# Float32r transposes of copied queries and keys, and probabilities transposed one step later

## The chip, the cores and the metric

The kernel runs on one core of one Trainium2 chip. The metric is the device time of one execution in microseconds; the program before takes 460.76 us (median of 3 runs, 460.70 to 461.07). TensorE, VectorE, ScalarE, GpSimd and SyncE are called PE, DVE, ACT, POOL and SP below, as in the profile.

## What is computed

One layer of a hybrid decoder: 512 tokens of width 1024, float32. A normalised input goes through one wide projection, whose columns feed a block-sparse attention branch (8 heads of 64) and a gated linear recurrence (4 heads of 128); both are up-projected, gated, merged, projected again, and a gated embedding is added.

```python
xn = rmsnorm(h, norm_gain[i])
proj = xn @ w_in[i]
aq, ak, av, ag, bq, bf, bi, bg, gate_a, gate_b = jnp.split(proj, split_pts, axis=-1)
qa = rmsnorm(heads(aq), q_norm_gain[i])
ka = rmsnorm(heads(ak), k_norm_gain[i])
ya = moba_attention(qa, ka, heads(av), rel_bias)      # softmax(q k^T * scale + bias) v, causal
ya = (ya * silu(ag)) @ w_up_a[i]
yb = hgrn2_chunkwise(silu(bq), kb, bi, log_f)
yb = (rmsnorm(yb, hgrn_out_gain[i]) * silu(bg)) @ w_up_b[i]
h = h + (sigmoid(gate_a) * ya + sigmoid(gate_b) * yb) @ w_out[i]
h = h + (p[i] @ w_ple[i]) * sigmoid(h @ w_ple_gate[i])
```

## The kernel before

Each large product is made of float32r matmuls on operands that are split in a high and a low part (hi·hi, hi·lo, lo·hi), 128x128 weights against 512 columns. `proj_tr` and `mm3` (L256) make one 128-row block of the projection from 24 such matmuls; `proj_tok` (L396) makes the value, query and key projections with tokens on partitions, in four PSUM banks of 128 tokens each: `bi`, `av`, `aq`, `ak`. Weights come by SP's transfers, ACT writes their high part (`wh`, L239) and DVE the low part (`wl`, L240), three buffers each.

The main stream on PE is a list of such blocks (`ORDER`): after `aq` and `ak` come `bg0`, `ag0`, `bf1`, `bq1`, `bg1` and so on, then `ub`, `ua`, `h` and the last gate. Into this stream side generators put their own work: the recurrence (score matmuls `lpb` and `lpa`, transposes `hktp`, state products `hds`, outputs `hop`), the normalisation of queries and keys (`qk_norm`), and attention. The stream counts estimated microseconds (`tick`, `cost`), and a generator that yields a number gets its turn when the count has passed it. PE's order is therefore the order in which the code is written out (`manual_schedule` for PE). ACT, DVE and POOL get their order from a scheduler that simulates the program at build time.

PSUM has four banks for the main stream (tag `mm`), two for the recurrence (`g`) and two for attention (`a`). The four `mm` banks go round: `ak0` to `ak3` hold the key projection, and `bg0`, `ag0`, `bf1`, `bq1` are written into those same banks, each after its `ak` has been copied out.

`qk_norm`, for queries and then for keys: ACT copies each bank to a tile (`qr` or `kr`, L636), squares it (`qq`, `kq`, L638), DVE sums the squares (L639), ACT and DVE make the inverse root (L267 to L272), DVE multiplies the tiles in place (L645). The raw query tiles stand in the buffers `P` and `PC` that attention uses later, the raw key tiles in `R`, which has four buffers of its own. PE transposes them as float32: four 128x128 transposes for each pair of heads, `qtp` (L658) four times in a row of turns, `ktp` (L674) once for each pair of heads as attention gets to it. Column 0 of the bias tiles of the first two heads is first written from the last key tile (L764), so that their load comes no sooner.

Attention has 24 steps (8 heads, query blocks (0, 1), (2), (3)). A step's scores (`s`, L700) go to one `a` bank; DVE adds the bias and takes the row maximum (L707), ACT exponentiates (L709). In the next step `divide` scales the probabilities (ACT, L722), and a transfer on ACT's queue copies them to a float32r tile (`pc`, L726). `LAG` steps after its scores, at 0.4 of the step, PE transposes `pc` (`pt`, L734), ACT copies the result (`ptS`, L738), and each pair of heads ends with the products with the values (`o`, L749).

The recurrence's end for head 0 matters below: PE makes `hop0` (L595, L597), ACT squares it (`ht0`, L603), and `column_norms` makes the norm: a transpose and a reduction on DVE (L332, L333), four small DVE operations (L334 to L337), the logarithm and exponential on ACT (`n16t` L267, `n16y` L268), more on DVE, and the output `ho0` (L605), which stands in a ring of eight buffers, `YB`.

Of the kernel before, what the change touches and what calls it, by code (L numbers as in the profile page):

```python
# [11 lines left out]
F32 = mybir.dt.float32  # L12
R = mybir.dt.float32r
# [8 lines left out]
NT = S // 128  # L22
# [8 lines left out]
STEPS = ((0, 1), (2,), (3,))  # L31

HP = 3.1
AP = 6.1
LAG = 2
H0 = 8.0
XN = 3.0

# [22 lines left out]
def hybrid_layer_kernel(  # L61
    ctx: ExitStack,
    tc: tile.TileContext,
    xT: bass.AP,
    pT: bass.AP,
    smalls: bass.AP,
    brow: bass.AP,
    masks: bass.AP,
    w_tok: bass.AP,
    w_tr: bass.AP,  # L70
# [6 lines left out]
    nc = tc.nc  # L77
    V, A, G, PE = nc.vector, nc.scalar, nc.gpsimd, nc.tensor
# [11 lines left out]
    def unit(tag, name, dt=F32, shape=(128, 512)):  # L90
        return sb.tile(list(shape), dt, tag=tag, bufs=BUFS[tag], name=name)

    def bank(tag, name):
        return psum.tile([128, 512], F32, tag=tag, bufs={"mm": 4, "g": 2, "a": 2}[tag], name=name)
# [34 lines left out]
    def cost(us):  # L129
        now[0] += us  # L130
# [26 lines left out]
    identr = cst.tile([128, 128], R, name="identr")  # L157
    G.tensor_copy(identr, identf[:, 0:128])
    ident = identr.bitcast(F32)
# [27 lines left out]
    def pin(op, engine="V"):  # L187

        if engine in pinned:
            tc.add_manual_dep(op.ins, pinned[engine].name,  # L190
                              mybir.DependencyInfo(mybir.DependencyClass.NoSync, mybir.DependencyReason.DATA))
        pinned[engine] = op.ins
# [5 lines left out]
    def scale_split(hi, lo, src, g):  # L198
        A.activation(hi, src, AF.Copy, scale=g)
        V.scalar_tensor_tensor(lo, src, g, hi.bitcast(F32), op0=OP.mult, op1=OP.subtract)  # L200
# [64 lines left out]
    def rsqrt(y, t, ms):  # L265

        A.activation(t, ms, AF.Ln, bias=epsc[0:t.shape[0], 0:1])  # L267
        A.activation(y, t, AF.Exp, scale=-0.5)  # L268
        V.scalar_tensor_tensor(t, ms, EPS, y, op0=OP.add, op1=OP.mult)
        V.tensor_tensor(t, t, y, op=OP.mult)  # L270
        V.tensor_scalar(t, t, -0.5, 1.5, op0=OP.mult, op1=OP.add)
        V.tensor_tensor(y, y, t, op=OP.mult)  # L272
# [356 lines left out]
    def qk_norm(name, banks, g, res):  # L629
        raws = []  # L630
        ss = cst.tile([128, NT, HEADS], F32, name=name + "ss")
        y = cst.tile([128, NT, HEADS], F32, name=name + "y")
        t_ = cst.tile([128, NT, HEADS], F32, name=name + "t")
        for t in range(NT):
            raw = unit(("P", "PC")[t % 2] if name == "q" else "R", f"{name}r{t}")
            A.activation(raw, banks[t], AF.Copy)  # L636
            sq = unit("PT", f"{name}q{t}")
            A.activation(sq, raw, AF.Square)  # L638
            V.tensor_reduce(ss[:, t], sq.rearrange("p (h d) -> p h d", h=HEADS), axis=AX.X, op=OP.add)  # L639
            raws.append(raw)  # L640
        V.tensor_scalar(ss, ss, 1.0 / 64, None, op0=OP.mult)
        rsqrt(y, t_, ss)
        for t in range(NT):
            r3 = raws[t].rearrange("p (h d) -> p h d", h=HEADS)
            V.tensor_tensor(r3, r3, y[:, t, :, None].to_broadcast([128, HEADS, 64]), op=OP.mult)  # L645
        yield 14.0
        if name == "q":
            yield from stacked_queries(raws, g, res)
        else:
            res.extend(raws)  # L650
        done.add(name)

    def stacked_queries(raws, g, res):

        for i in range(HPAIRS):
            tp = bank("a", f"qtp{i}")
            for t in range(NT):
                PE.transpose(tp[:, t * 128:t * 128 + 128], raws[t][:, i * 128:i * 128 + 128], ident)  # L658
            cost(0.44)
            with tc.high_priority(offset=AHEAD):  # L660
                for j in range(2):
                    qs = unit("A", f"qs{2 * i + j}", R)
                    own, other = slice(64 * j, 64 * j + 64), slice(64 - 64 * j, 128 - 64 * j)
                    A.activation(qs[own], tp[own], AF.Copy, scale=g[own])
                    V.scalar_tensor_tensor(qs[other], tp[own], g[own], qs[own].bitcast(F32),
                                           op0=OP.mult, op1=OP.subtract)
                    res.append(qs)
            yield 1.5

    def doubled_keys(raws, i):  # L670

        tp = bank("a", f"ktp{i}")
        for t in range(NT):
            PE.transpose(tp[:, t * 128:t * 128 + 128], raws[t][:, i * 128:i * 128 + 128], ident)  # L674
        cost(0.44)
        res = []
        for j in range(2):
            kh = unit("A", f"kh{2 * i + j}", R)
            kl = unit("A", f"kl{2 * i + j}", R)
            own, other = slice(64 * j, 64 * j + 64), slice(64 - 64 * j, 128 - 64 * j)  # L680
            with tc.high_priority(offset=AHEAD):
                scale_split(kh[own], kl[own], tp[own], kgain[own])
            for k_ in (kh, kl):
                nc.sync.dma_start(k_[other].bitcast(F32), k_[own].bitcast(F32))
            res.append((kh, kl))
        return res

    def attention(qn, kraw, va, sags, res):
# [24 lines left out]
        def divide(n):  # L713


            if n not in prs:
                return
            with tc.high_priority(offset=AHEAD):
                for _, st in scaled:
                    pin(V.reciprocal(st[:, 2:3], st[:, 1:2]))  # L720
                for p_, st in scaled:
                    A.activation(p_, p_, AF.Copy, scale=st[:, 2:3])  # L722
                h, i = steps[n]
                w = 128 * sum(qb + 1 for qb in STEPS[i])
                c = unit("PC", f"pc{h}{i}", R)
                nc.scalar.dma_start(c[:, 0:w].bitcast(F32), prs[n][:, 0:w])  # L726
                prs[n] = c
            scaled.clear()

        def transposed(h, qbs, pr):  # L730
            n = sum(qb + 1 for qb in qbs)
            tp = bank("a", f"pt{h}{qbs[0]}")
            for kb in range(n):
                PE.transpose(tp[:, kb * 128:kb * 128 + 128].bitcast(R), pr[:, kb * 128:kb * 128 + 128], identr)  # L734
            cost(0.06 * n)
            pt = unit("PT" if n == NT else f"PT{qbs[0]}", f"ptS{h}{qbs[0]}", shape=(128, n * 128))
            with tc.high_priority(offset=AHEAD):
                A.activation(pt, tp[:, :n * 128], AF.Copy)  # L738
            return pt
# [21 lines left out]
        def bias(h):  # L761
            t = unit("T", f"bias{h}")
            if h < 2:
                V.tensor_copy(t[:, 0:1], kraw[NT - 1][:, 0:1])  # L764
            row = brow[h:h + 1, :]
            nc.sync.dma_start(t, bass.AP(tensor=row.tensor, offset=row.offset, ap=[[1, 128], [1, 512]]))
            return t

        while not {"q", "k"} <= done:
            yield lambda: {"q", "k"} <= done  # L770
        T = {0: bias(0), 1: bias(1)}
        kn += doubled_keys(kraw, 0)
        yield 7.0
        NS = len(STEPS)
        steps = [(h, i) for h in range(HEADS) for i in range(NS)]
        prs, pts = {}, {}
        pending = None
        for n in range(len(steps) + LAG + 1):
            divide(n - 1)
            if pending is not None:  # L780
                while f"ag{pending}" not in done:
                    yield lambda: f"ag{pending}" in done
                out_values(pending, pts)
                pending = None
            if n < len(steps):
                h, i = steps[n]
                prs[n] = scores(h, STEPS[i], T[h])
                if i == 1 and h + 2 < HEADS:
                    T[h + 2] = bias(h + 2)
                if i == 1 and h % 2 and h + 1 < HEADS:  # L790
                    yield 1.0
                    kn += doubled_keys(kraw, h // 2 + 1)
                yield AP * (0.4 if n >= LAG else 0.8)
            if LAG <= n < len(steps) + LAG:
                h, i = steps[n - LAG]
                pts[h, i] = transposed(h, STEPS[i], prs.pop(n - LAG))
                if i == NS - 1 and h % 2:
                    pending = h // 2
                yield AP * 0.6

    def drain(name):

# [245 lines left out]
    for at, n in enumerate(PAIRS):  # L1048
# [24 lines left out]
        if at in (2, 3):  # L1073
            t = unit("A", f"pf{at}")
# [12 lines left out]
    for p in range(4):  # L1087
        pes = [bank("ag"[p % 2], f"pe{p}{i}") for i in range(2)]
        a, b, c, d = (bank("mm", f"g{i}{p}") for i in "abcd")
# [186 lines left out]
```

## Time and profile before

| | |
|---|---|
| runs | 460.70, 460.76, 461.07 us |
| profiled execution | 461.04 us, of which the span from the first to the last instruction is 459.0 us |
| mean granted TensorE clock | 0.999 |
| PE busy | 99% of the span |
| DVE busy | 74% |
| ACT busy | 64% |
| DMA | 55.69 MB, mean 121 GB/s |

The profile was taken from one execution. Busy time counts from an instruction's start to its end; matmuls overlap, so the pace of PE is read from the starts: the 512-column matmuls of the main stream start 0.23 us apart. In the timelines a row has the start, the duration, the engine, the line and operation, output<-inputs, shapes, a count, and in brackets the engine's idle time before it and what ended that.

### The profile page before, as it was taken

The numbers are of one execution on the slowest core, as the hardware profiler recorded it, in microseconds if no ns is written. First come the engines' busy times: TensorE is split into PE (matmuls) and PEld (weight loads), VectorE is DVE, ScalarE is ACT, GpSimd is POOL, SyncE is SP. The second block draws the span as 40 slices with busy tenths as digits, with TensorE's granted clock in tenths as the row PEclk, the third lists the DMA queues.
The fourth block names the chain that finished last, engine by engine and source line by source line (L and its number), as shares of the span: only waits on it lengthen the run. The fifth ranks groups of instructions, "written<-read, shape, count | busy, mean of one in ns | idle before, by whom it ended". The sixth has DMA issues, their size and how long they took to land.

```text
span 459.0 us, 7767 instructions
## 1 busy us (share of the span) xinstructions
PE 453.2 (99%) x2903; PEld 383.1 (83%) x2903; DVE 341.4 (74%) x715; ACT 294.3 (64%) x538; POOL 14.3 (3%) x35
## 2 busy tenths in 40 slices
PE   8999999999999999999999999999999999999996
PEld 6888888888888888888878888888888888899996
DVE  4889567869979877978897556233548968899885
ACT  5856665658688987979696866766434435557331
POOL 1005000000000000001000000000000000000000
PEclk9999999999999999999999999999999999999999
DMA  7642322321443533442523344213423534463112
GB/s 253 213 142 78 107 91 95 99 84 57 158 131 112 158 106 133 131 134 88 160 89 124 119 125 162 63 64 109 133 92 111 175 129 161 160 202 120 47 47 93
DMA packets 23061, 55.69 MB, mean 121 GB/s; under 512 B 2800, under 2 KB 5744, under 8 KB 23024
## 3 DMA queue, kind: packets, MB, share of 16 engines
q1 hardware_dynamic: 19424, 49.95, 33.8%
q10 hardware_dynamic: 3600, 5.25, 3.1%
q8 instruction: 23, 0.38, 0.3%
q14 instruction: 14, 0.11, 0.1%
HBM read 45.75 MB, written 2.10 MB: 104 GB/s over the span
## 4 chain that ended last, share of the span: by engine, by line
PE 96%; DMA 2%; ACT 1%; issue 0%; DVE 0%; SPq 0%; DVEq 0%
PE ga L256 10%; PE gb L256 10%; PE h L256 10%; PE ub L256 5%; PE ak L396 5%; PE bq L256 5%; PE ua L256 5%; PE ag L256 5%; PE bf L256 5%; PE aq L396 5%; PE av L396 5%; PE bi L396 4%; PE bg L256 4%; PE pe L1103 2%; PE ga L1112 2%; PE gc L1112 2%
## 5 line engine op out<-in xcount | busy, mean ns | idle before, releaser
L240 DVE TENSOR_TENSOR wl<-wf,wh 128x1024 fp32r<-128x1024 f32 (+1 forms) x70 | 77.6, 1110 | 39.4 <-ACT wh L239 38.3
L239 ACT ACTIVATE wh<-wf 128x1024 fp32r<-128x1024 f32 (+1 forms) x70 | 67.1, 959 | 58.8 <-PE h L256 9.8
L256 PE MATMUL gb<-xh,wh 128*128 128x512 f32 x64 | 25.8, 403 | 0.0
L256 PE MATMUL ga<-xh,wh 128*128 128x512 f32 x64 | 25.6, 400 | 0.0
L256 PE MATMUL gb<-xh,wl 128*128 128x512 f32 x64 | 25.1, 392 | 0.0
L256 PE MATMUL ga<-xh,wl 128*128 128x512 f32 x64 | 25.0, 391 | 0.0
L256 PE MATMUL gb<-xl,wh 128*128 128x512 f32 x64 | 25.0, 391 | 0.0
L256 PE MATMUL ga<-xl,wh 128*128 128x512 f32 x64 | 25.0, 390 | 0.0
L256 PE MATMUL h<-ml,wh 128*128 128x512 f32 x64 | 25.0, 390 | 0.0
L256 PE MATMUL h<-mh,wl 128*128 128x512 f32 x64 | 24.9, 389 | 0.0
L256 PE MATMUL h<-mh,wh 128*128 128x512 f32 x64 | 24.9, 389 | 0.0
L707 DVE CUSTOM_DVE_ANT_0 p<-s,bias 128x128 f32<-128x128 f32 (+3 forms) x32 | 15.0, 486 | 11.5 <-PE s L700 10.9
L709 ACT ACTIVATE p<-p,ps 128x128 f32<-128x128 f32 (+3 forms) x32 | 17.7, 555 | 7.4 <-DVE ps L707 7.2
L722 ACT ACTIVATE p<-p,ps 128x128 f32<-128x128 f32 (+3 forms) x32 | 17.0, 553 | 6.4 <-DVE ps L720 6.3
L738 ACT ACTIVATE ptS<-pt 128x384 f32<-128x384 f32 (+1 forms) x24 | 12.5, 520 | 6.6 <-PE pt L734 6.4
L256 PEld LDWEIGHTS h<-ml,wh 128*128 128x128 f32 x64 | 12.0, 188 | 2.7 <-DVE ml L196 0.2
L256 PEld LDWEIGHTS gb<-xh,wl 128*128 128x128 f32 x64 | 12.0, 188 | 2.7
L256 PEld LDWEIGHTS ga<-xh,wl 128*128 128x128 f32 x64 | 12.0, 188 | 2.7
L256 PEld LDWEIGHTS h<-mh,wh 128*128 128x128 f32 x64 | 12.0, 188 | 2.5
L256 PEld LDWEIGHTS h<-mh,wl 128*128 128x128 f32 x64 | 12.0, 188 | 2.4
L256 PEld LDWEIGHTS ga<-xh,wh 128*128 128x128 f32 x64 | 12.0, 187 | 2.3
L256 PEld LDWEIGHTS ga<-xl,wh 128*128 128x128 f32 x64 | 12.0, 188 | 2.2
(412 smaller groups left out, 1406.7 us busy)
## 6 DMA issues: line engine op xcount, KB each, us to landing
wf<-in_w_tr_dram SPq DMA_DIRECT2D x32, 512.0 KB, 3.3
wf<-in_w_tok_dram SPq DMA_DIRECT2D x15, 512.0 KB, 3.3
wf<-in_w_up_dram SPq DMA_DIRECT2D x16, 256.0 KB, 2.6
wf<-in_w_o_dram SPq DMA_DIRECT2D x8, 512.0 KB, 3.3
pc<-p ACTq DMA_DIRECT2D x16, 192.0 KB, 2.8
bias<-in_brow_dram SPq DMA_DIRECT2D x8, 256.0 KB, 3.8
pc<-p ACTq DMA_DIRECT2D x8, 256.0 KB, 2.7
xres<-in_xT_dram SPq DMA_DIRECT2D x8, 256.0 KB, 3.1
```

The costliest lines, as they stand in the source:

```text
L239: A.activation(hi, wraw[i], AF.Copy)
L240: pin(V.tensor_tensor(lo, wraw[i], hi.bitcast(F32), op=OP.subtract))
L256: PE.matmul(ps, a[:, k, :], b[k], start=(n == 0), stop=(n == tot - 1))
L396: PE.matmul(banks[t], a[:, s_], b[:, kk, :], start=(k == 0 and i == 0), stop=(k == KD - 1 and i == 2))
L707: V.tensor_tensor_reduce(p_, sp[:, o:o + nk], T[:, nk - 1::-1], -1.0, 3e38, OP.add, OP.min, st[:, 0:1])
L709: A.activation(p_, p_, AF.Exp, bias=st[:, 0:1], scale=-1.0, accum_out=st[:, 1:2])
L722: A.activation(p_, p_, AF.Copy, scale=st[:, 2:3])
L738: A.activation(pt, tp[:, :n * 128], AF.Copy)
L1103: PE.matmul(pes[i][:, cols], wt[:, i, k, :], t[k][:, cols], start=k == n == 0, stop=k == 1 and n == 2 and (bool(parts) or cols == right))
L1112: PE.matmul(dst[:, left], wt[:, k, :], bt, start=begin and n == 0, stop=n == 11, skip_group_check=not begin)
```

## The change

There are two parts.

1. **Queries and keys.** The raw tiles `qr` and `kr` move to the ring `YB` (eight buffers, four for each of the two). After the multiplication by the inverse root, a transfer on ACT's queue copies each tile to a float32r tile: `qc` in `P` and `PC`, `kc` in `R`, where the raw tiles were. The transposes read these copies, with the float32r identity, and write a float32r view of the bank. The tile that gates the first two bias loads is now `kc3`.
2. **Attention's order.** `LAG` goes from 2 to 3, and the transposes of probabilities stand at the head of a step, ahead of the division and the scores, with no turn of the main stream between them and the scores. `AP`, the counted length of a step, goes from 6.1 to 6.4.

```diff
-AP = 6.1
-LAG = 2
+AP = 6.4
+LAG = 3
...
         for t in range(NT):
-            raw = unit(("P", "PC")[t % 2] if name == "q" else "R", f"{name}r{t}")
+            raw = unit("YB", f"{name}r{t}")
...
             V.tensor_tensor(r3, r3, y[:, t, :, None].to_broadcast([128, HEADS, 64]), op=OP.mult)
+            c = unit(("P", "PC")[t % 2] if name == "q" else "R", f"{name}c{t}", R)
+            nc.scalar.dma_start(c.bitcast(F32), raws[t])
+            raws[t] = c
...
-                PE.transpose(tp[:, t * 128:t * 128 + 128], raws[t][:, i * 128:i * 128 + 128], ident)
-            cost(0.44)
+                PE.transpose(tp[:, t * 128:t * 128 + 128].bitcast(R), raws[t][:, i * 128:i * 128 + 128], identr)
+            cost(0.24)
...
-                V.tensor_copy(t[:, 0:1], kraw[NT - 1][:, 0:1])
+                V.tensor_copy(t[:, 0:1], kraw[NT - 1][:, 0:1].bitcast(F32))
...
         for n in range(len(steps) + LAG + 1):
-            divide(n - 1)
             if pending is not None:
...
+            if LAG <= n < len(steps) + LAG:
+                h, i = steps[n - LAG]
+                pts[h, i] = transposed(h, STEPS[i], prs.pop(n - LAG))
+                if i == NS - 1 and h % 2:
+                    pending = h // 2
+            divide(n - 1)
             if n < len(steps):
...
-                yield AP * (0.4 if n >= LAG else 0.8)
-            if LAG <= n < len(steps) + LAG:
-                h, i = steps[n - LAG]
-                pts[h, i] = transposed(h, STEPS[i], prs.pop(n - LAG))
-                if i == NS - 1 and h % 2:
-                    pending = h // 2
-                yield AP * 0.6
+                yield AP * (1.0 if n >= LAG else 0.8)
+            else:
+                yield AP * 0.5
```

The same edit of the transposes stands in `stacked_queries` (queries) and `doubled_keys` (keys). What the order of the engines makes of this is shown at three places. The line numbers of the changed kernel are 3 to 4 higher than those of before from L645 on.

On ACT, before, at the end of the key projection: the copies of the key banks `ak0` to `ak2` (`kr0` to `kr2`) stand between the query tiles `qs`, ahead of `ht0`.

```order
L636 ACTIVATE kr0_1139<-ak0_786 128x512
L664 ACTIVATE qs4_1052<-qtp2_1047,qgain_92 64x512
L638 ACTIVATE kq0_1141<-kr0_1139 128x512
L636 ACTIVATE kr1_1144<-ak1_787 128x512
L664 ACTIVATE qs5_1055<-qtp2_1047,qgain_92 64x512
L664 ACTIVATE qs6_1077<-qtp3_1072,qgain_92 64x512
L638 ACTIVATE kq1_1146<-kr1_1144 128x512
L636 ACTIVATE kr2_1149<-ak2_788 128x512
L664 ACTIVATE qs7_1080<-qtp3_1072,qgain_92 64x512
L638 ACTIVATE kq2_1151<-kr2_1149 128x512
L603 ACTIVATE ht0_1098<-hop0_1089 128x512
L239 ACTIVATE wh20_1128<-wf20_1126 128x1024
```

The same place on ACT now:

```order
L667 ACTIVATE qs7_1088<-qtp3_1080,qgain_92 64x512
L603 ACTIVATE ht0_1109<-hop0_1100 128x512
L239 ACTIVATE wh20_1136<-wf20_1134 128x1024
L267 ACTIVATE n16t_109<-n16s_107,epsc_79 32x16
L268 ACTIVATE n16y_108<-n16t_109 32x16
L636 ACTIVATE kr0_1147<-ak0_786 128x512
L636 ACTIVATE kr1_1152<-ak1_787 128x512
L636 ACTIVATE kr2_1157<-ak2_788 128x512
L636 ACTIVATE kr3_1162<-ak3_789 128x512
L638 ACTIVATE kq0_1149<-kr0_1147 128x512
```

All four copies of key banks now stand behind `n16t` and `n16y` of the recurrence's norm. In the program `kr0` itself waits for nothing; the first matmul into `bg0` waits for ACT's count up to and with `kr0`, whose bank it takes.

On DVE now, the operations that make the input of `n16t`, from the transpose of `ht0` on, with the low part of weight block 20 among them:

```order
L332 STREAM_TRANSPOSE h0nu_1111<-ht0_1109 128x512
L333 TENSOR_REDUCE n16s_107<-h0nu_1111 128x16
L240 TENSOR_TENSOR wl20_1137<-wf20_1134,wh20_1136 128x1024
L334 TENSOR_TENSOR n16s_107<-n16s_107 32x16
L335 TENSOR_TENSOR n16s_107<-n16s_107 32x16
L336 TENSOR_TENSOR n16s_107<-n16s_107 32x16
L337 TENSOR_SCALAR n16s_107<-n16s_107 32x16
L269 SCALAR_TENSOR_TENSOR n16t_109<-n16s_107,n16y_108 32x16
```

Before, two operations on the squares of keys (`kss`) stood between these; they now come behind `ho0`.

On PE, around the transposes of the probabilities of head 3, query block 2 (`pt32`), before: they stand 12 main-stream matmuls behind the scores of their second next step, and alone.

```order
L256 MATMUL bg3_2537<-xl7_412,wh36_2390 128x512
L256 MATMUL bg3_2537<-xh7_411,wl36_2391 128x512
L734 MATMUL pt32_2591<-identr_88,pc31_2488 128x128 x3
L256 MATMUL ag3_2608<-xh0_380,wh37_2468 128x512
L256 MATMUL ag3_2608<-xl0_381,wh37_2468 128x512
```

The same place now:

```order
L256 MATMUL bg3_2569<-xl4_399,wh36_2406 128x512
L256 MATMUL bg3_2569<-xh4_398,wl36_2407 128x512
L737 MATMUL pt32_2598<-identr_88,pc31_2429 128x128 x3
L703 MATMUL s42_2610<-kh4_2341,qs4_1060 128x384
L703 MATMUL s42_2610<-kl4_2342,qs4_1060 128x384
L256 MATMUL bg3_2569<-xh5_402,wh36_2406 128x512
```

They now stand directly ahead of the scores of the third next step. From the scores at whose step the division was made (`s33`) to `pt32` there were 42 main-stream matmuls, one score group and one group of transposes; now there are 54, with a score group, a group of transposes and the `hop` products.

More of the change, by code (lines that the diff above doesn't have):

```diff
@@ L673, in doubled_keys @@
         for t in range(NT):
-            PE.transpose(tp[:, t * 128:t * 128 + 128], raws[t][:, i * 128:i * 128 + 128], ident)
-        cost(0.44)
+            PE.transpose(tp[:, t * 128:t * 128 + 128].bitcast(R), raws[t][:, i * 128:i * 128 + 128], identr)
+        cost(0.24)
         res = []
```

## The prediction

> **What bounds the kernel now.** I read the busy times and the chain of the page first, then the waits of PE.
>
> ```profile
> PE 453.2 (99%) x2903; PEld 383.1 (83%) x2903; DVE 341.4 (74%) x715; ACT 294.3 (64%) x538; POOL 14.3 (3%) x35
> ...
> PE 96%; DMA 2%; ACT 1%; issue 0%; DVE 0%; SPq 0%; DVEq 0%
> ```
>
> ```profile
> PE pt L734 <- DMA pc<-p: 0.8, 1, 0.8
> ```
>
> PE works all the time: 96% of the chain is PE, and behind the first microseconds its waits hold one idle stretch, before transposes of probabilities. So an edit counts by what it does to PE's sequence of starts: a shorter instruction is a gain, and a wait of PE is a loss in full, because no idle time comes later that could take it up.
>
> **The change part by part.**
>
> *Type of the transposes.* 32 transposes go from float32 to float32r, in eight groups of four. Neither kind is new to the trace. A group of keys (`ktp`) as it is, and a group of four probabilities (`pt`), each between 512-column matmuls:
>
> ```profile
> 125.21 0.40 PE L256 MATMUL bf<-xh,wl 128*128 128x512 f32 x1
> 125.44 0.60 PE L674 MATMUL ktp<-identr,kr 128*128 128x128 f32 x4
> 125.80 0.48 PE L256 MATMUL bf<-xh,wh 128*128 128x512 f32 x1
> 126.11 0.40 PE L256 MATMUL bf<-xl,wh 128*128 128x512 f32 x1
> ```
>
> ```profile
> 189.33 0.40 PE L256 MATMUL ag<-xh,wl 128*128 128x512 f32 x1
> 189.56 0.46 PE L734 MATMUL pt<-identr,pc 128*128 128x128 f32 x4
> 189.86 0.46 PE L256 MATMUL ag<-xh,wh 128*128 128x512 f32 x1
> 190.16 0.40 PE L256 MATMUL ag<-xl,wh 128*128 128x512 f32 x1
> ```
>
> From the matmul ahead of the group to the second one behind it: 126.11 - 125.21 = 0.90 us in float32, 190.16 - 189.33 = 0.83 us in float32r. The difference, 0.075 us before rounding of the starts, times eight is **-0.60 us**, about 0.30 of it in the four query groups, which all stand ahead of `bg0`. (The program's own estimates, 0.44 and 0.24, would say -1.6; the trace decides.)
>
> *Transposes one step later.* The idle stretch:
>
> ```profile
> 235.37 0.39 PE L256 MATMUL bg<-xh,wl 128*128 128x512 f32 x1
> 236.54 0.42 PE L734 MATMUL pt<-identr,pc 128*128 128x128 f32 x3 [0.78 <-DMA pc<-p]
> ```
>
> The start comes 1.17 us after the one before, where 0.23 is usual: 0.94 us lost to the copy of `pc` landing late. This is `pt32`. Between the division and it stood 42 main-stream matmuls, now 54 and a `hop`: at 0.23 us each, 2.8 us more before `hop` is counted. That is more than was missing, so I count **-0.94 us**; next late is nothing that the trace of before shows waiting. Joining transposes and scores changes the number of PE's instructions by none, and I cost it at nothing. A bound on the gain is the delay that a transpose leaves behind it, 190.16 - 189.86 = 0.30 against 0.23, 0.07 us times 24, or -1.7; but it is only passed to the score that follows. A bound on the loss is below, with the rivals.
>
> *The copies as transfers.* Eight more transfers on ACT's queue.
>
> ```profile
> L726 ACTq DMA_DIRECT2D pc<-p x24: 472/472/524, 143.1 to 334.1; - x24
> ...
> DMA to landing us min/median/max: 2.1/2.7/4.5
> ```
>
> ```profile
> 94.36 0.27 ACT L552 ACTIVATE sc<-lpb 64x128 f32<-64x128 f32 x1
> ...
> L658 PE MATMUL qtp<-identr,qr x16: 272/273/273, 97.8 to 106.0; 128*128 128x128 f32 x16
> ```
>
> Each issue holds ACT's queue for 0.47 us. The last query copy, `qc3`, stands just ahead of the `sc` copy of the second row, so it is issued at about 94.4 and lands at 97.1 by the median; the first `qtp` starts at 97.8. It hides, with 0.7 us to spare; by the slowest landing it costs 1.1. I take nothing. SP's order changes by a place or two in a few loads that run ahead; nothing.
>
> The key copies come behind the wait of the next part, which holds PE up as well. From that part: the copy of the last key bank starts at about 116.0, `bg0` at 114.8. Before:
>
> ```profile
> 111.81 0.58 ACT L636 ACTIVATE kr<-ak 128x512 f32<-128x512 f32 x1
> ...
> 117.85 1.27 DVE L645 TENSOR_TENSOR kr<-kr,ky 128x512 f32<-128x512 f32 x2
> ```
>
> From that copy to the last product 7.3 us passed (111.81 to 119.12); the rest of `ho0`, some 3 us on DVE as an estimate, may now come between. With issue and landing `kc3` is there at 126.5 to 129.7. `ktp0`, 66 matmuls behind `bg0`'s start, is due at 130.0 or later. DVE does wait for `kc3` at the first bias's gate; behind it stand `bg0s` and `wl22`, which `bg1` needs 36 matmuls later, at 138. Nothing is lost by them.
>
> *The key banks.* This is the part that decides. The first matmul into `bg0` waits for `kr0`, the copy of bank `ak0`. Before, that copy was long done:
>
> ```profile
> 103.76 0.60 ACT L636 ACTIVATE kr<-ak 128x512 f32<-128x512 f32 x1
> ...
> 110.37 0.60 ACT L603 ACTIVATE ht<-hop 128x512 f32<-128x512 f32 x1
> 110.86 1.05 ACT L239 ACTIVATE wh<-wf 128x1024 fp32r<-128x1024 f32 x1
> ...
> 115.46 0.29 ACT L267 ACTIVATE n16t<-n16s,epsc 32x16 f32<-32x16 f32 x1
> 115.79 0.22 ACT L268 ACTIVATE n16y<-n16t 32x16 f32<-32x16 f32 x1
> 115.91 1.04 ACT L239 ACTIVATE wh<-wf 128x1024 fp32r<-128x1024 f32 x1
> ```
>
> ```profile
> 109.24 1.39 PE ak L396 x6
> ...
> 110.24 0.39 PE L396 MATMUL ak<-wl,xh 128*128 128x512 f32 x1
> 110.47 0.39 PE L256 MATMUL bg<-xh,wh 128*128 128x512 f32 x1
> ```
>
> Now `kr0` stands on ACT behind `ht0`, `wh20`, `n16t` and `n16y`, and `n16t` needs six operations of DVE after `ht0`. Rows of DVE for the chain:
>
> ```profile
> 111.11 0.70 DVE L332 STREAM_TRANSPOSE h0nu<-ht 128x512 f32<-128x512 f32 x1
> 111.95 1.23 DVE L240 TENSOR_TENSOR wl<-wf,wh 128x1024 fp32r<-128x1024 f32 x1
> 113.09 0.68 DVE L333 TENSOR_REDUCE n16s<-h0nu 128x16 f32<-128x512 f32 x1
> 113.68 0.68 DVE L639 TENSOR_REDUCE kss<-kq 128x8 f32<-128x512 f32 x1
> 114.38 0.17 DVE L334 TENSOR_TENSOR n16s<-n16s 32x16 f32<-32x16 f32 x1
> ...
> 114.76 0.18 DVE L641 TENSOR_SCALAR kss<-kss 128x32 f32<-128x32 f32 x1
> 114.97 0.16 DVE L336 TENSOR_TENSOR n16s<-n16s 32x16 f32<-32x16 f32 x1
> ```
>
> PE first. Before, `hop0` ended and the last six `ak` began at 109.24, and `bg0` started at 110.47. Now the queries save 0.30, and three of the six `ak` stand ahead of `hop0`, so `hop0` ends at 109.24 - 0.30 + 0.68 = 109.62, and PE would start `bg0` at 110.17. ACT, without the key work between, is free and starts `ht0` at 109.67. From that start: 0.74 to the start of L332 (110.37 to 111.11), 0.70 for it, 0.59 for L333 (113.09 to 113.68), 1.14 for `wl20` (111.95 to 113.09), 0.87 from L334 to `n16t` (114.38 to 115.46, less the 0.21 of L641, which is gone), 0.33 to `n16y`, 0.12 to what follows it, 0.60 for `kr0`: 5.09 us. `kr0` ends at 114.76, `bg0` starts at 114.8: **+4.6 us** of waiting. `wh20` does not lengthen it (it would let `wl20` start sooner than L333 does). By waits that I cannot see between dependent operations it may be 4.3 to 5.0. The three other banks are copied 0.6 us apart behind `kr0`, sooner than PE needs them.
>
> *The clock.* No row of before has PE idle for so long in its midst, but the kernel's end has:
>
> ```profile
> 455.10 0.28 PE L1103 MATMUL pe<-ph,pwl 128*128 128x256 f32 x1
> ...
> 455.40:457.60 2.20, 0.00 (x0) 0.00 (x0) 0.84 (x2) 0.00 (x0) 0.00 (x0) 1.00 0.41 138
> 457.70:459.00 1.30, 0.00 (x0) 0.00 (x0) 0.00 (x0) 0.00 (x0) 0.00 (x0) 0.50 0.00 0
> ```
>
> ```profile
> 0.77 3.39 PE L150 MATMUL warm<-const-float32-1.0 128*128 128x128 f32 x16 [0.77 <-PEq L1263]
> ...
> 103.80 0.67 PE hds L582 x6
> ```
>
> In the two window rows the third figure from the end is the granted clock: 1.00 up to 2.2 us after PE's last matmul (455.10 + 0.28), then 0.50. So an idle stretch of more than 4 us can bring it down. At the start, the same form of matmul ran at 3.39/16 = 0.21 us, against 0.67/6 = 0.11 later: half pace for some 3.4 us of work until the full clock came. If that repeats behind the wait, the work of 3.4 us is done at half pace, and the loss is **+1.7 us**; none if the clock stays, 3.4 if it takes such a stretch twice. I take 1.7, by the row of the start.
>
> [...] The row here, at most 2.3 us, speaks for the drop.
>
> **Sum.** The profiled execution took 461.04 us: 461.04 - 0.60 - 0.94 + 4.6 + 1.7 = 465.8. It was 0.28 us over the median of the runs, 460.76, so a median of **465.5 us** follows.
>
> **Rivals.**
>
> 1. *The wait comes, the clock stays.* For it: the drop at the end is one event, and the wait is not much longer than twice that idle time. 465.5 - 1.7 = 463.8 us.
> 2. *More is lost.* The half pace lasts for a second such stretch (+1.7, 467.2), or new waits come: `qc3` landing late (1.1), or `ptS` not ready when a `ktp` needs its bank (in two places `ktp` now comes two score matmuls and six others behind a `pt`, 1.8 us at 0.23 each; ACT has rows of 1.05 us that can stand between). One or two of these with the forecast give 466.5 to 468.5.
> 3. *Faster.* ACT is not held by `n16t`, so that `kr0` is copied in time as before, and only the gains are left: 460.76 - 0.60 - 0.94 = 459.2 us. It decides at a wait of 1.5 us in all: below it the kernel is faster. Against it: `kr0` is behind `n16t` on the same queue, and before, ACT's rows start in the order listed (103.76, 110.37, 110.86). The chain of 5.09 us would have to shrink by 3.1.
> 4. *The type does not shorten the transposes* (the price is in the move, not in the type): +0.60, 466.1, inside the range.
>
> **How the numbers follow.** The forecast has 62%, with the fourth case in it; the first rival 15%, the second 17%, the third 4%; 2% are for a result near the old time, if half the wait is covered by something unseen. The range takes the first rival and the lower half of the second: 463.4 to 467.6 us. Faster by more than 0.2% (0.9 us, about what a measurement of this kernel can tell from no change): 4%; within: 3%; slower: 93%.
>
> **What would show it.** Right: PE idle for 4.3 to 5.0 us before `bg0`, put down to ACT's `kr`, with ACT idle before `n16t`; a granted clock of 0.50 for some microseconds from there; `qtp` and `ktp` groups 0.075 us shorter; no wait of `pt` for `pc`. Wrong: a `bg0` that starts within 1.5 us of the last `ak`; matmuls at 0.23 us straight behind the wait (then rival 1); waits of `ktp` or `qtp` on ACT or on `qc` (then rival 2).

## The result, and the profile after

The changed kernel takes **465.43 us** (median of 5 runs, 465.31 to 466.63) against 460.76 before: a ratio of 1.0107, 95% interval 1.0095 to 1.0120. It is slower by 1.1%. The profiled execution is the longest of the five, 466.63 us, with a span of 464.6 us; so the trace shows a little more loss than the median holds.

The page of the changed kernel, its busy times and its chain, hardly differs from before: PE is still the bound.

```profile
PE 455.2 (98%) x2903; PEld 384.9 (83%) x2903; DVE 340.8 (73%) x715; ACT 295.3 (64%) x538; POOL 14.5 (3%) x35
...
PE 96%; DMA 1%; DVE 1%; SPq 0%; issue 0%; ACT 0%; DVEq 0%
```

PE's busy time rose by 2.0 us with the same 2903 matmuls, and its span by 5.6. The first says that matmuls have become slower somewhere, the rest that PE stands still. The waits of PE name the place (engine, line, what it waited for: total us, times, longest):

```profile
PE bg L256 <- ACT kr L636: 4.4, 1, 4.4
```

The wait of `pt` for `pc` is gone from this view. The timeline of PE at the new wait:

```profile
109.92 0.40 PE L396 MATMUL ak<-wl,xh 128*128 128x512 f32 x1
114.74 0.80 PE L256 MATMUL bg<-xh,wh 128*128 128x512 f32 x1 [4.42 <-ACT kr L636]
115.33 0.63 PE L256 MATMUL bg<-xl,wh 128*128 128x512 f32 x1
115.76 0.63 PE L256 MATMUL bg<-xh,wl 128*128 128x512 f32 x1
...
120.45 0.45 PE L256 MATMUL bg<-xl,wh 128*128 128x512 f32 x1
120.74 0.39 PE L256 MATMUL bg<-xh,wl 128*128 128x512 f32 x1
```

From the last `ak` to `bg0` it is 4.82 us from start to start, where 0.23 is usual: 4.59 us lost. Behind the wait the starts are 0.43 apart (115.33 to 115.76) until about 120.5. The windows of the same stretch (length; busy time and count of PE, PEld, DVE, ACT and POOL; granted clock; DMA) say why:

```profile
109.90:113.70 3.80, 0.41 (x2) 0.00 (x0) 3.24 (x8) 1.46 (x3) 0.00 (x0) 1.00 0.00 0
113.80:117.10 3.30, 2.36 (x6) 1.90 (x7) 2.52 (x10) 3.27 (x8) 0.13 (x1) 0.50 0.48 159
117.20:120.50 3.30, 3.30 (x10) 2.56 (x9) 3.06 (x6) 1.29 (x3) 0.20 (x1) 0.50 0.00 0
120.60:124.00 3.40, 3.40 (x17) 2.77 (x16) 2.81 (x8) 1.14 (x3) 0.00 (x0) 1.00 0.06 21
```

PE gets half the clock for 6.8 us and then the full one. What PE waits for is seen on ACT:

```profile
109.66 0.60 ACT L603 ACTIVATE ht<-hop 128x512 f32<-128x512 f32 x1 [0.49 <-PE hop L597]
110.28 1.06 ACT L239 ACTIVATE wh<-wf 128x1024 fp32r<-128x1024 f32 x1
113.66 0.31 ACT L267 ACTIVATE n16t<-n16s,epsc 32x16 f32<-32x16 f32 x1 [2.32 <-DVE n16s L337]
113.99 0.22 ACT L268 ACTIVATE n16y<-n16t 32x16 f32<-32x16 f32 x1
114.12 2.00 ACT L636 ACTIVATE kr<-ak 128x512 f32<-128x512 f32 x4
```

ACT itself is idle for 2.32 us ahead of `n16t`, while the four copies of key banks stand behind it, though the matmuls that fill the last of these banks had ended at 110.32. DVE works through that time on the input of `n16t`, with a low part of weights in the middle:

```profile
110.29 0.71 DVE L332 STREAM_TRANSPOSE h0nu<-ht 128x512 f32<-128x512 f32 x1 [0.33 <-ACT ht L603]
111.03 0.69 DVE L333 TENSOR_REDUCE n16s<-h0nu 128x16 f32<-128x512 f32 x1
111.64 1.22 DVE L240 TENSOR_TENSOR wl<-wf,wh 128x1024 fp32r<-128x1024 f32 x1
112.88 0.16 DVE L334 TENSOR_TENSOR n16s<-n16s 32x16 f32<-32x16 f32 x1
```

To see where time goes in all the kernels, the table has four stretches of each profiled execution, by the first starts of PE's stages (`aq`, `bg0`, `ag0`, `h`) and the end of its last matmul. The key wait lies in the first stretch, the clock in the second, nearly all of attention in the third. What comes ahead of `aq` varies by up to 0.8 us from one execution to the next and is left out.

| kernel | median, us | `aq` to `bg0` | `bg0` to `ag0` | `ag0` to `h` | `h` to the end |
|---|---|---|---|---|---|
| before | 460.76 | 49.96 | 5.44 | 246.15 | 93.32 |
| changed | 465.43 | 54.24 | 8.31 | 244.68 | 93.30 |
| own place for `ho` | 458.59 | 49.68 | 5.48 | 244.73 | 93.22 |
| the same, again | 458.73 | 49.59 | 5.47 | 244.78 | 93.26 |
| attention alone | 459.52 | 49.93 | 5.44 | 244.81 | 93.25 |
| queries and keys alone | 466.04 | 54.23 | 7.21 | 244.98 | 93.27 |
| 19 matmuls in the wait | 464.86 | 54.23 | 5.62 | 245.32 | 93.29 |
| changed, again | 466.00 | 54.24 | 7.85 | 244.76 | 93.24 |
| 19 matmuls, again | 466.73 | 54.29 | 5.61 | 245.75 | 93.22 |
| 10 matmuls in the wait | 465.01 | 54.20 | 7.19 | 244.80 | 93.22 |
| own place, float32 | 459.57 | 49.92 | 5.48 | 244.96 | 93.22 |
| transposes apart | 458.73 | 49.68 | 5.47 | 244.59 | 93.22 |
| later step alone | 459.71 | 49.96 | 5.44 | 245.17 | 93.28 |

Changed against before: +4.28, +2.87, -1.47 and -0.02, together 5.66 us.

### The profile page after: what moved, and what is told of

Same layout as the page of the kernel before. It is cut to its first block, busy times and chain, and to the rows that moved or that the text cites. A ratio compares the mean times of both kernels' runs of the same rounds, so it can differ in the third digit from the quotient of the medians.

```text
span 464.6 us, 7783 instructions
## 1 busy us (share of the span) xinstructions
PE 455.2 (98%) x2903; PEld 384.9 (83%) x2903; DVE 340.8 (73%) x715; ACT 295.3 (64%) x538; POOL 14.5 (3%) x35
## 4 chain that ended last, share of the span: by engine, by line
PE 96%; DMA 1%; DVE 1%; SPq 0%; issue 0%; ACT 0%; DVEq 0%
PE gb L256 9%; PE ga L256 9%; PE h L256 9%; PE bg L256 5%; PE ub L256 5%; PE bf L256 5%; PE bq L256 5%; PE aq L396 5%; PE ag L256 5%; PE ua L256 5%; PE av L396 5%; PE ak L396 5%; PE bi L396 4%; PE s L703 3%; PE pe L1107 2%; PE ga L1116 2%
## 5 line engine op out<-in xcount | busy, mean ns | idle before, releaser
L256 PE MATMUL bg<-xh,wh 128*128 128x512 f32 x32 | 13.9, 433 | 4.4 <-ACT kr L636 4.4
```

Of the source, the lines that this page charges most:

```text
L256: PE.matmul(ps, a[:, k, :], b[k], start=(n == 0), stop=(n == tot - 1))
```

## The experiments

The first theory: the key copies were pushed behind the recurrence's norm because raw keys and the output `ho0` now share the ring `YB`; the wait and the clock after it are the whole loss, and the rest of the change is a gain.

### A place of its own for `ho`

```diff
-    BUFS = {"w": 2, "wh": 3, "wl": 3, "A": 16, "R": 4, "X": 16,
+    BUFS = {"w": 2, "wh": 3, "wl": 3, "A": 16, "R": 4, "HO": 1, "X": 16,
...
-            o = unit("YB", f"ho{h}")
+            o = unit("HO", f"ho{h}")
```

> The change with one edit: the recurrence's outputs ho stand in a buffer of their own instead of the ring YB, in which the raw key tiles had to follow ho0. In the program the copies of the key banks then stand ahead of ht0 on ACT, as before the change. Theory (the loss is bg0's wait for kr0 and the half clock behind it): no wait before bg0, clock 0.999, 460.76 - 0.60 - 0.94 = 459.2 us (458.9 to 459.8). Rival A (the loss comes from the eight transfers on ACT's queue, the landing of qc3 and kc3 and DVE's wait at the bias gate, all of which stay): 463 to 465.5 us. Rival B (attention's new order loses, which also stays): above 461 us.

Measured: 458.59 us (458.24 to 458.74), a little under the expected range, before beside it 460.84; ratio 0.9952, 0.9940 to 0.9965. ACT and PE of this kernel:

```profile
103.13 0.60 ACT L636 ACTIVATE kr<-ak 128x512 f32<-128x512 f32 x1
...
107.53 0.58 ACT L636 ACTIVATE kr<-ak 128x512 f32<-128x512 f32 x1
...
109.50 0.60 ACT L603 ACTIVATE ht<-hop 128x512 f32<-128x512 f32 x1
```

```profile
109.34 0.40 PE L396 MATMUL ak<-wl,xh 128*128 128x512 f32 x1
109.57 0.40 PE L256 MATMUL bg<-xh,wh 128*128 128x512 f32 x1
```

The copies of the first three banks are back ahead of `ht0`, `bg0` follows `ak` after 0.23 us, and the clock is 1.0 in all runs. Nothing else was edited, so the shared ring is what moved the copies; by which rule the scheduler lets the ring do so was not looked into. The whole loss goes, and the kernel is faster than both.

### Each part alone

Attention's later step alone, with queries and keys as before; and the reverse, where attention's loop has its old order. Both diffs are shown in part and stand against the changed kernel: in the first the transposes go back to float32 as well, in the second the transposes of probabilities go back to half a step behind the scores.

```diff
-            raw = unit("YB", f"{name}r{t}")
+            raw = unit(("P", "PC")[t % 2] if name == "q" else "R", f"{name}r{t}")
...
-            c = unit(("P", "PC")[t % 2] if name == "q" else "R", f"{name}c{t}", R)
-            nc.scalar.dma_start(c.bitcast(F32), raws[t])
-            raws[t] = c
...
```

> Before, with the attention part of the change alone (LAG 3, AP 6.4, transposes at a step's head); queries and keys as before, in float32 and without transfers. Theory: the idle stretch before pt32 is gone (-0.94) and nothing comes but the wait of the scores s13 for the bank of ktp1, about 0.28 us in the trace of the changed kernel: 459.8 to 460.2 us. Rival (the joined transposes and scores lose time of their own in the 24 steps): 460.8 us or more.

```diff
-AP = 6.4
-LAG = 3
+AP = 6.1
+LAG = 2
...
```

> Before, with the part on queries and keys alone (raw tiles in YB, copies by transfer, float32r transposes); attention as before with LAG 2. Theory: the wait of bg0 is 4.4 to 4.8 us and the clock halves for some microseconds, as in the changed kernel; 460.76 + 4.6 + 1.3 to 2.5 - 0.6 = 466.1 to 467.3 us, less 0.9 if the idle stretch before pt32 goes because everything else has caught up. Rival B (attention's order makes the loss): 460.2 us.

Attention alone: 459.52 us (458.96 to 459.83), ratio 0.9974 (0.9962 to 0.9985), no wait; that is 0.3 us under the expected range, and the 0.28 us expected for a bank is not among the waits. Queries and keys alone: 466.04 us (465.64 to 466.39), ratio 1.0116 (1.0100 to 1.0131), with the same wait of 4.4 us before `bg0`. The loss belongs to the key part. The attention part alone gains 1.34 us in the third stretch; on top of the other part it adds 0.30 (244.98 to 244.68).

Two readings did not fit what I had thought. The kernel with queries and keys alone keeps `LAG` at 2, and yet PE does not wait at `pt32`. Its trace gives the near cause: the copy of these probabilities was issued at 232.96, 7.8 us ahead of the transposes at 240.75, where before it was 4.3 us (232.26 to 236.54), as the division now stands sooner among ACT's work. Why the scheduler put it there is open. That the engines made up ground while PE stood still before `bg0` is not the reason in the kernels with the later step: the changed kernel, with that wait, and the kernel with its own place for `ho`, without it, both issue this copy 8.03 us ahead. In the changed kernel it is issued at 232.54, and the group of transposes one step earlier starts at 233.01. The copies of `pc` there took 2.1 us at least, so in this order the later step was needed. And attention alone gained 1.34 us in the third stretch, not 0.94; I put the rest down to the joining of transposes and scores, which the prediction had at nothing. The last experiments test that.

The windows of queries and keys alone show half pace for one stretch only:

```profile
114.80:118.10 3.30, 3.30 (x8) 2.58 (x9) 3.06 (x9) 2.26 (x5) 0.42 (x2) 0.50 0.16 65
118.30:121.80 3.50, 3.50 (x17) 2.85 (x16) 2.60 (x8) 1.63 (x4) 0.00 (x0) 1.00 0.00 0
```

### The clock by itself: matmuls in the wait

The changed kernel with 512-column matmuls between `ak` and `bg0`, which write into a bank that nobody reads, so that PE is busy while it waits.

```diff
+FILL = 19
...
+    filler = bank("g", "filler")
+    for _ in range(FILL):
+        PE.matmul(filler, identr, xh[0], start=True, stop=True)
```

> The change with 19 more 512-column matmuls between ak and bg0, into a bank that nothing reads: 19 x 0.227 = 4.3 us of work for PE in place of 4.3 us of the idle 4.6. The wait of bg0 for kr0 stays where it is, the clock should not halve. Theory (the wait and the half clock are two separate terms, and idleness of PE brings the clock down): faster than the changed kernel by the clock's loss, 1.2 to 2.5 us, 463.3 to 464.3 us, clock 0.999, though it does more work. Rival (the clock has no part in it, or falls for another reason): 465.2 to 466 us, or longer by what the fill exceeds the wait.

Measured: 464.86 us (464.17 to 465.21), ratio 1.0087 (1.0073 to 1.0101), the clock 1.0 in all four runs. PE's timeline:

```profile
109.83 4.59 PE L894 MATMUL filler<-xh,identr 128*128 128x512 f32 x19
114.42 0.50 PE L258 MATMUL bg<-xh,wh 128*128 128x512 f32 x1
114.76 0.40 PE L258 MATMUL bg<-xl,wh 128*128 128x512 f32 x1
```

`bg0` starts no sooner, 54.23 us behind `aq`, but goes at the full pace: 5.62 us to `ag0` in place of 8.31. That separates the two terms in the trace. The median is half a microsecond above the expected range, though, and the third stretch is 0.64 longer than in the changed kernel; 0.35 of that is one stop of PE, which is shown below for the second run. So three kernels were run together: the changed one again, 19 matmuls again, and 10, which end well ahead of the wait's end.

> The changed kernel once more, beside the two fills on one chip. The clock's loss depends on how the wait falls on the steps in which the clock is granted: one step of 3.41 us at half pace (clock 0.995 or 0.996, about 465.4 us) or two (0.993, about 466.5 us). Theory: the runs fall into these two groups, 465.2 to 465.9 and 466.2 to 466.8 us. Rival (the spread has nothing to do with the clock): no gap between the groups, and times that do not go with the clock.

> The fill of 19 matmuls once more, since its median of 464.86 us lay above the 463.3 to 464.3 us expected. Theory (the wait is unchanged, only the clock's loss goes): faster than the changed kernel of the same job by 1.2 to 1.8 us on the median, and in the trace bg0 to ag0 takes 5.6 us, against 7.2 or 8.3. Rival (the fill gives back part of it elsewhere): faster by less than 0.9 us, with the difference behind ag0 in the trace.

> The change with 10 fill matmuls: PE works for 2.3 us of the wait and is idle for some 2.2 us before bg0. Theory (an idle stretch of about 2.2 us is at the edge at which the clock falls, since it fell 2.2 us after the last matmul at the end of the kernel before): most runs keep clock 0.999, time as with 19, 464.0 to 465.0 us. Rival (what counts is that PE waits at all): the clock falls as without the fill, 465.3 us or more.

Changed again: 466.00 us (465.84 to 466.48), ratio 1.0115 (1.0102 to 1.0128). 19 matmuls again: 466.73 us (464.59 to 467.75, 4 runs), ratio 1.0137 (1.0122 to 1.0151). 10 matmuls: 465.01 us (463.28 to 465.50, 6 runs), ratio 1.0083 (1.0068 to 1.0098).

All three expectations failed in part. The changed kernel did not fall into two groups: all four executions have a mean clock of 0.993, that of two steps, and their times, 465.84, 465.93, 466.08 and 466.48, run from the first expected group through the gap into the second. So the mean clock alone does not give the time; the last section shows why. The kernel with 19 matmuls had `bg0` to `ag0` at 5.61 us as expected, but was 0.7 us slower than the changed kernel instead of 1.2 to 1.8 faster. With 10 matmuls four executions of six lost the full clock, where most were expected to keep it.

As a median 19 matmuls gave no gain the second time, so as a remedy they failed. Part of it is in the trace: in the second run PE stops between two `lpa` matmuls for something the profile can't name.

```profile
257.09 0.55 PE L544 MATMUL lpa<-hqx,hkx 128*32 128x48 f32 x32
257.43 0.46 PE L546 MATMUL lpa<-hq,hk 128*32 128x48 f32 x24
258.29 0.29 PE L546 MATMUL lpa<-hq,hk 128*32 128x48 f32 x8 [0.39 <-issue]
```

Both runs with 19 matmuls have this stop at the same matmul, the one with 10 has not. It doesn't explain the executions of 466.59 and 466.86 us at a full clock and of 467.75 at 0.996, of which there is no trace; what took 2 us and more there stays open.

The kernel with 10 matmuls is the clean measurement, since its six executions fall in two groups by the mean granted clock: 1.0 in those of 463.28 and 463.45 us, 0.996 in those of 464.85, 465.16, 465.35 and 465.50. The means are 463.37 and 465.22: one drop of the clock cost 1.85 us here. By this pair, and by the traces with 19 matmuls, the half pace is a cost beside the wait. Its profiled execution is one of the second group:

```profile
109.55 2.49 PE L894 MATMUL filler<-xh,identr 128*128 128x512 f32 x10
114.14 0.50 PE L258 MATMUL bg<-xh,wh 128*128 128x512 f32 x1 [2.10 <-ACT kr L638]
```

```profile
112.50:115.50 3.00, 1.36 (x6) 1.14 (x7) 2.04 (x11) 2.41 (x7) 0.00 (x0) 1.00 0.48 175
115.70:119.00 3.30, 3.30 (x9) 2.59 (x8) 3.16 (x6) 2.08 (x4) 0.42 (x2) 0.50 0.00 0
119.30:121.00 1.70, 1.70 (x9) 1.42 (x8) 0.95 (x5) 0.55 (x2) 0.00 (x0) 1.00 0.00 0
```

Here the clock falls 1.48 us after PE has gone back to work (114.14 to 115.62, by the trace's record of the clock), and an idle time of 2.1 us was enough.

### The type

The kernel with its own place for `ho`, with copies and transposes in float32 (diff against that kernel, in part; the same edit of the transposes stands for queries and for keys).

```diff
-            c = unit(("P", "PC")[t % 2] if name == "q" else "R", f"{name}c{t}", R)
-            nc.scalar.dma_start(c.bitcast(F32), raws[t])
+            c = unit(("P", "PC")[t % 2] if name == "q" else "R", f"{name}c{t}")
+            nc.scalar.dma_start(c, raws[t])
...
-                PE.transpose(tp[:, t * 128:t * 128 + 128].bitcast(R), raws[t][:, i * 128:i * 128 + 128], identr)
+                PE.transpose(tp[:, t * 128:t * 128 + 128], raws[t][:, i * 128:i * 128 + 128], ident)
```

> The kernel with ho in a buffer of its own, in which queries and keys are copied by transfers as in the change, but into float32 tiles, and transposed as float32. Theory: eight groups of four cost 0.90 instead of 0.83 us each, so 458.6 + 0.6 = 459.2 us, and the groups in the trace show it. Rival (the copy brings or costs something beside the type): the groups are as long as in float32r, or the time moves by other than 0.4 to 0.8 us.

Measured: 459.57 us (459.27 to 459.83, 7 runs), ratio 0.9973 (0.9963 to 0.9984). Against 458.59 and 458.73 of the float32r kernel, run beside other runs of before, that is 0.8 to 1.0 us; by the table 0.24 in the first stretch and 0.23 in the third (against the first run), 0.47 in all, where 0.60 was predicted. A group of key transposes takes 125.87 - 124.96 = 0.91 us in its trace, from the matmul ahead of it to the second one behind, as long as before. Of the rest of the difference the profiled executions show 0.26 to 0.38 us ahead of `aq`, which is in no stretch of the table; why the medians lie more than the expected 0.4 to 0.8 us apart is not settled. The first stretch of the float32 kernel, 49.92 us, is that of before, 49.96: the transfers themselves cost PE nothing there. By the stretches the type is worth about half a microsecond.

### Joining transposes and scores, and the later step

> The changed kernel with a place of its own for the output of hop, a second time, as the base of the two that run beside it: 458.6 us (458.2 to 459.2), 244.7 us from the first matmul of ag to the first of h, no wait of PE behind the first microsecond. If the first run of it was a lucky one, 459.2 as the prediction's terms without a wait give.

The second, against the first:

```diff
+GAP = 0.65
...
                     pending = h // 2
+                if n < len(steps):
+                    yield GAP
             divide(n - 1)
...
-                yield AP * (1.0 if n >= LAG else 0.8)
+                yield AP * 0.8 if n < LAG else AP - GAP
```

> The same kernel, but in each step three 512-column matmuls stand between the transposes of the probabilities and the scores. Theory: where transposes are followed by the score and not by a matmul of the main stream, one slow second start of about 0.03 us is saved, 24 times; parted again, this costs 0.67 us: 0.5 to 0.8 us over the run beside it, about 459.3, and about 245.4 us from the first ag to the first h. Rival: joining them saves nothing, as the prediction had it, and the gain came from something else; then this kernel takes the time of the run beside it within 0.2 us.

The third is the kernel before with `LAG = 3` and three buffers for `PC`, nothing else.

> The kernel before, with the transposes of the probabilities one step later and three buffers for their copies, and nothing else: transposes still stand half a step behind the scores, and queries and keys are as before. Theory: only the idle 0.94 us ahead of the transposes of step 32 goes: 460.8 - 0.94 = 459.8 us (459.6 to 460.1), about 245.2 us from the first ag to the first h, against 246.15 before. Rival: the later step is worth the whole 1.3 us that the attention part gained, and joining nothing: 459.5 us, 244.8 us. Second rival: the idle time comes back elsewhere, 460.8 us, with a wait of pt for pc or of a matmul for a bank in the trace.

Measured, beside the same runs of before (460.60): own place again 458.73 us (458.60 to 459.19); apart 458.73 us (458.38 to 459.31), both with a ratio of 0.9961 (0.9948 to 0.9973); later step alone 459.71 us (459.00 to 460.30, 11 runs), 0.9981 (0.9972 to 0.9990).

My theory on the joining falls: parted, the kernel takes the same time, and its third stretch is 0.19 us shorter, not 0.67 longer. PE in the joined kernel (first) and in the parted one (second), at a group of four transposes:

```profile
189.87 0.40 PE L256 MATMUL ag<-xh,wl 128*128 128x512 f32 x1
190.11 0.46 PE L737 MATMUL pt<-identr,pc 128*128 128x128 f32 x4
190.41 0.46 PE L703 MATMUL s<-kh,qs 128*128 128x512 f32 x1
190.71 0.40 PE L703 MATMUL s<-kl,qs 128*128 128x512 f32 x1
```

```profile
244.43 0.40 PE L257 MATMUL ga<-xh,wl 128*128 128x512 f32 x1
244.66 0.46 PE L738 MATMUL pt<-identr,pc 128*128 128x128 f32 x4
244.96 0.46 PE L257 MATMUL ga<-xh,wh 128*128 128x512 f32 x1
245.26 0.40 PE L257 MATMUL ga<-xl,wh 128*128 128x512 f32 x1
```

The second start behind a group of transposes comes 0.30 us after the first, whether it is a score (190.71) or a matmul of the main stream (245.26). The delay goes with the transposes, as the prediction put it.

The later step alone is 0.89 us faster by the medians and 0.98 by the third stretch, without a wait at `pt32`:

```profile
237.39 0.40 PE L256 MATMUL ag<-xh,wl 128*128 128x512 f32 x1
237.62 0.38 PE L734 MATMUL pt<-identr,pc 128*128 128x128 f32 x3
```

So the 0.94 us can be had by one number and one buffer. Why attention alone gained 0.36 more than this in the third stretch is not settled; the joining in itself does not do it in the float32r kernel, and `AP`, which is 6.4 there and 6.1 here and so sets how much of the main stream stands between two steps, was not tried by itself.

A ring of their own for the raw keys was not tried.

## Why the prediction was right

The sign, the place and the mechanism were right, and the size was close: 465.5 us forecast, 465.43 measured, 466.00 in a second set. In part that closeness is luck, as the items on the key banks and the clock show. Step by step:

- **Type, -0.60.** Right for a group, a little large in sum. A group of keys between 512-column matmuls in the changed kernel takes 133.18 - 132.34 = 0.84 us (0.833 before the starts are rounded), against the 0.83 forecast; taken away alone, the type is worth 0.47 by the stretches. Not all eight groups stand between such matmuls.

```profile
132.34 0.40 PE L256 MATMUL bf<-xh,wl 128*128 128x512 f32 x1
132.58 0.46 PE L677 MATMUL ktp<-identr,kc 128*128 128x128 f32 x4
132.88 0.46 PE L256 MATMUL bf<-xh,wh 128*128 128x512 f32 x1
133.18 0.40 PE L256 MATMUL bf<-xl,wh 128*128 128x512 f32 x1
```

- **The idle time before `pt32`, -0.94.** Right: 0.98 with the later step alone. The forecast did not see that it depends on ACT's order too: with queries and keys alone it went without the later step.
- **Joining, nothing.** Right to within 0.2 us, though I doubted it in between.
- **Copies as transfers, nothing.** Right. The last query copy was issued at 93.27 us, about 1 us sooner than the 94.4 forecast, and transfers of `qc` took 3.1 us at most; `qtp` began at 97.84. The gate on DVE waited for `kc3` as foreseen, 1.50 us, and no matmul for it:

```profile
127.08 0.21 DVE L767 COPY bias<-kc 128x1 f32<-128x1 f32 x2 [1.50 <-DMA kc<-kr]
```

- **The key banks, +4.6.** Right: 4.59 from start to start, in the changed kernel, with `ht0` at 109.66 (109.67 forecast), `kr0` at 114.12 and `bg0` at 114.74 (114.8). Each of the parts of the chain was a duration that the trace of before had, only in another order. Single parts were off by up to 0.11 us both ways (0.63 for 0.74 to the start of L332, 1.24 for 1.14 at `wl20`); that they cancel in the sum is luck. The experiment with `ho` in its own place took away exactly this wait.
- **The clock, +1.7.** The mechanism is right and the size is that of one stretch of half pace: 1.85 us by the two groups with 10 matmuls, 7.21 - 5.44 = 1.77 in the trace of queries and keys alone. The row of the start from which it was taken could not give it: in the trace of before the full clock came at 3.65 us, 2.9 us after the first of the 16 matmuls (0.77), and in the other twelve traces between 3.98 and 6.59. The profiled execution had two stretches, 2.87 us; that is why it is 0.8 us over the 465.8 of the sum, which the other terms would put 0.3 under it. In the first set three of the five executions had a mean clock of 0.995 or 0.996 and took 465.31 to 465.43 us, two had 0.993 and took 466.27 and 466.63; in the second set all four had 0.993 and took 465.84 to 466.48. So one stretch, as forecast, came in three executions of nine, and two in six, going by the mean clock. That the median of the first set is one of the three is luck: the two kinds of execution are 0.4 to 1.3 us apart, and either may hold the middle.

Of the rivals, the first (the clock stays, 463.8) is what the two full-clock executions with 10 matmuls show: 463.28 and 463.45. It did not come because the clock did fall. The second is in part what six of the nine executions show, a second stretch of half pace; they took 465.84 to 466.63, under its 467.2, since part of the first stretch fell into the wait (1.00 and 1.96 us of it in the two that were profiled), where PE had nothing to lose. Its new waits did not come. The third (no wait, 459.2) is the kernel with its own place for `ho`, 458.59 and 458.73 us. By the sum of the table's four stretches it saves 1.76 us against before, where 1.54 was worked out; what else makes its median lower is not settled.

## What to carry to other kernels

Before moving a tile to another ring of buffers, look at who else takes buffers there and what the scheduler then puts ahead of it on the same engine: here one shared ring put a copy that was ready behind a chain of 5 us, and one extra buffer gave it back. For a wait of PE of some microseconds look at the granted clock behind it too: here 4.6 us of waiting before `bg0` cost 6.4 us (queries and keys alone) to 7.5 us (changed). A part that gains and a part that loses can be told apart by running each alone; of this change the better version keeps both and undoes only the sharing, 458.6 us.

## What was not expected of the hardware

The clock moved in steps. By the trace's record of the granted clock, half pace behind the wait lasted 3.41 us (queries and keys alone, 10 matmuls) or 6.83 us (changed, both times), nothing else. The times from the full clock to the drop are multiples of 3.41 us as well: 109.23 us in the changed kernel and 105.81 in its second set, 32 and 31 steps, and 453.97 us in the trace of before, 133 steps. In these traces the loss is half of the time that PE works at half pace: in the changed kernel half pace began at 113.74, 1.00 us ahead of `bg0`, and (6.83 - 1.00) / 2 = 2.9 us, measured 2.87; in its second set it began at 112.40 with `bg0` at 114.36, (6.83 - 1.96) / 2 = 2.4 us, measured 2.41; with queries and keys alone it began at 114.78, 0.14 behind `bg0`, and 3.41 / 2 = 1.7, measured 1.77.

Where the drop lay against the wait differed: it came 1.00 and 1.96 us ahead of `bg0` where two steps of 3.41 us went at half pace, and 0.14 and 1.48 us behind it where one did. From these four traces I estimate that how an idle time falls on the steps decides whether none, one or two of them go at half pace, which would explain why executions of one kernel differ; no run tests that by itself. In the two traces with two steps PE was idle for the first 1.00 and 1.96 us of the first step and the full clock did not come at its end; it came at the end of the next, in which PE was at work throughout. Four traces don't make this a rule. How much idle time brings a drop was not measured: 2.10 us did in the profiled execution with 10 matmuls, and before the change 0.78 us at `pt32` did not (clock 1.00 on both sides of it).

The drop came at no fixed time after PE's last matmul: half pace began 3.42 us after its end in the changed kernel (110.32 to 113.74), 2.46 us after it in the second set (109.94 to 112.40) and 2.25 us after it at the end of the kernel before (455.38 to 457.63).
